# Gate-tile sums tied to a place in VectorE's queue, and pooling blocks spread over projection blocks, in a one-core transformer block

## The chip, the cores and the metric

The kernel runs on one core of one Trainium2 chip. The metric is the time of one execution in device microseconds (us); three executions of the kernel before the change gave 2939.7, 2941.09 and 2943.04, median 2941.09. One more execution was recorded by the profiler and is the source of every row below.

## The reference, cut to what matters

One layer of a diffusion backbone in float32, with 256 latent tokens, 256 context tokens and 4096 channels:

```
mod  = silu(c) @ w_ada + b_ada              -> shift, scale, gate    (w_ada: 4096 x 12288)
h    = rmsnorm(x) * (1 + scale) + shift     (the context likewise, from c_ctx)
xa, xb, ga, gb = split(h @ w_in)            (w_in: 4096 x 16384; the context needs xa alone)
ya   = RG-LRU(xa): convolution, two gates per head and direction, two scans (16 heads)
z    = centred_mean(xb, window 2, 4, 8, 16) - xb      (4 groups of 1024 channels)
yb   = (z @ w_pool[group] + b_pool) * pool_scale
x    = x + gate * ([ya * silu(ga), yb * silu(gb)] @ w_out)           (w_out: 8192 x 4096)
out  = rmsnorm(x) * g_final
```

## The kernel before

Float32 weights are split on the core into two float32r tiles. `load_w` (L101 to L109) starts a transfer of one 128x1024 weight tile into a `raw` buffer on SyncE's queue (L97), lets ScalarE write the high half `hi` (L104) and VectorE the low half `lo = raw - hi` (L106; for the first 139 tiles GpSimd does it). TensorE multiplies with `hi` and with `lo`. There are 9 buffers for `raw`, 4 for `hi` and 3 for `lo` (`RAWB, HIB, LOB`). A weight tile is called a unit here; the kernel has 843 of them.

The whole program is one list of events, which `run` walks: "w" events eat a weight tile, "a" events eat a tile that goes straight into a sum, "s" events do other work. `run` loads 5 weight tiles (`LOOK`) and 4 "a" tiles (`LOOK_A`) ahead. A scheduler then places the recorded instructions in each engine's queue; it keeps dependencies, but may put an instruction earlier or later than it was written. Each engine takes its own queue in order, so an instruction that waits holds up all that is queued behind it on that engine.

After a first stage (up to about 860 us, the same in both kernels) come two stages:

- **Projection** (to 2196 us). A block is 8 units that fill two PSUM tiles (`block_units`, matmuls L613 and L614); there are 16 blocks for `xb`, 16 for `gb`, 16 for `ga`. The blocks of `xb` come in four groups; each block's result is folded and pooled on ScalarE and VectorE (`evac_x`) into eight tiles `z` per group. A group's pooling products are four blocks of two units each (`prods`, weights `w_pool`, the same lines L613 and L614, reading `z`); each fills two PSUM tiles, which a copy on ScalarE (L587) and an addition on VectorE (L592) then empty into `yb`. There are four PSUM tiles for these blocks in all (`ps_mm`). A group's four pooling blocks stand in a row after the first `DELAY` = 12 units of the next group. The LRU pieces of 16 heads are spread over the whole stage; each has two weight tiles of its own (L522 to L524).
- **Output** (2196 to 2921 us). 8 blocks of 32 units (`out_units`); a unit is twelve matmuls, four each on L796 (high half), L797 (low half) and L798.

The gate vector is computed on VectorE: 4 groups of 32 tiles of `w_ada`, each tile multiplied by one column and added into a `wide` tile (`gate_units`, `accumulate`, L223, L225, and L231 for the last tile). Group 0 is spread over the end of the projection, groups 1 to 3 over 0.03 to 0.83 of the output stage (`GATE3`). A group's result is needed late, at unit 24 of the output block that uses it (`gate_row`, L762).

Of the kernel before, what the change touches and what calls it, by code (L numbers as in the profile page):

```python
# [15 lines left out]
KT = D // P  # L16
# [1 line left out]
T2 = 2 * T  # L18
HEADS = 16
KEEP = 8  # L20
DELAY = 12
GATE3 = (0.03, 0.83)
GATE_FROM, GATE_END = 0.9, 0.99
SPILL_Y = 12
GATE_AT = 24
# [17 lines left out]
W = 1024  # L43
# [25 lines left out]
def block_kernel(ctx, tc, xc, cvec, vecs, consts, w_ss, w_gate, w_xa, w_lat0, w_lat2, w_lat, w_pool, w_rec, w_out, xn, rows, out):  # L69
# [13 lines left out]
    def slot(name, dt=F32):  # L83
        return spool.tile([P, 512], dt, name=name, tag="s")

    def temp(name, dt=F32):
        return tpool.tile([P, 512], dt, name=name, tag="t")
# [4 lines left out]
    def wide_tile():  # L92
        return ps_2.tile([P, 1024], F32, name="wide", tag="wide")

    def load_raw(src):
        t = rawp.tile([P, W], F32, name="raw", tag="raw")[:, :src.shape[-1]]
        nc.sync.dma_start(out=t, in_=src)  # L97
        return t

    def load_w(src, eng=None):  # L100
        raw = load_raw(src)  # L101
        width = src.shape[-1]
        hi = hip.tile([P, W], F32R, name="hi", tag="hi")[:, :width]
        act.copy(out=hi, in_=raw)  # L104
        lo = lop.tile([P, W], F32R, name="lo", tag="lo")[:, :width]
        ins = (eng or dve).tensor_tensor(out=lo, in0=raw, in1=hi.bitcast(F32), op=SUB)  # L106
        if eng is not None:
            lo_ins.append(ins)
        return hi, lo  # L109

    lo_ins, used = [], [0]

    def run(events):
        queues = {}
        for kind, look in (("w", LOOK), ("a", LOOK_A)):
            queues[kind] = [[e for e in events if e[0] == kind], [], 0, look]
        for e in events:
            if e[0] == "s":
                e[1]()
                continue  # L120
            for kind in ("w", "a"):
                q = queues[kind]
                q[2] += e[0] == kind
                while len(q[1]) < min(len(q[0]), q[2] + q[3]):
                    n = q[0][len(q[1])]
                    q[1].append(load_w(n[1], n[3]) if kind == "w" else load_raw(n[1]))
            q = queues[e[0]]
            r, q[1][q[2] - 1] = q[1][q[2] - 1], None
            e[2](r)
# [4 lines left out]
    def A_(src, f):  # L134
        return ("a", src, f)

    def S_(f):
        return ("s", f)
# [79 lines left out]
    def accumulate(raw, j, width, k, accs, nv, part, fins, first, last):  # L218
        seg = raw[:, j * width:(j + 1) * width]
        for v in range(nv):  # L220
            s = sc6[:, k, 2 + v:3 + v]
            if first:
                dve.tensor_scalar(out=accs[v][:, :width], in0=seg, scalar1=s, scalar2=None, op0=MUL)  # L223
            elif not last:
                dve.scalar_tensor_tensor(out=accs[v][:, :width], in0=seg, scalar=s, in1=accs[v][:, :width],  # L225
                                         op0=MUL, op1=ADD)
            else:
                for h in range(width // part):
                    fin = temp("fin")
                    cut = slice(h * part, (h + 1) * part)  # L230
                    dve.scalar_tensor_tensor(out=fin[:, :part], in0=seg[:, cut], scalar=s, in1=accs[v][:, cut],  # L231
                                             op0=MUL, op1=ADD)
                    fins[h, v] = fin
# [43 lines left out]
    def gate_units(grp):  # L277
        st = {}

        def unit(k):  # L280
            def f(raw):
                if k == 0:
                    st["accs"] = [wide_tile()]
                    st["fin"] = {}
                accumulate(raw, 0, W, k, st["accs"], 1, 512, st["fin"], k == 0, k == KT - 1)
            return A_(w_gate[grp, k], f)

        return [unit(k) for k in range(KT)], st
# [41 lines left out]
    ya_sp = [dram.tile([P, 512], F32, name=f"ya_sp{h}") for h in range(HEADS)]  # L330

    def xa_units(c):
        k0, n = chunk_kt[c]
        per = W // n // P

        def unit(i):
            def f(w):
                used[0] += 1
                hi, lo = (t.rearrange("p (k m) -> p k m", k=n) for t in w)
                for j in range(per):  # L340
                    o = i * per + j
                    ps = mm_tile()
                    for k in range(n):
                        a, b = hc[k0 + k]
                        wh, wl = hi[:, k, j * P:(j + 1) * P], lo[:, k, j * P:(j + 1) * P]
                        pe.matmul(out=ps, lhsT=wh, rhs=a, start=(k == 0), stop=False)  # L346
                        pe.matmul(out=ps, lhsT=wh, rhs=b, start=False, stop=False)  # L347
                        pe.matmul(out=ps, lhsT=wl, rhs=a, start=False, stop=(k == n - 1))  # L348
                    if c == 0:
                        acc[o] = slot("acc")  # L350
                        act.copy(out=acc[o], in_=ps)
                    elif c < NC - 1 and o % 4 < POOL_ADDS:
                        part = temp("part")
                        act.copy(out=part, in_=ps)  # L354
                        nc.gpsimd.tensor_tensor(out=acc[o], in0=acc[o], in1=part, op=ADD)  # L355
                    else:
                        dve.tensor_tensor(out=acc[o], in0=ps, in1=acc[o], op=ADD)
                    if c == NC - 1 and o >= 2 * KEEP:
                        nc.sync.dma_start(out=xa_sp[o], in_=acc[o])
                        acc[o] = None  # L360
            return W_(w_xa[xa_base[c] + i], f, nc.gpsimd)
        return [unit(i) for i in range(32 // per)]
# [96 lines left out]
    for c in range(NC):  # L459
        main = xa_units(c)  # L460
        if c == 0:
            main = spread(main, ahead_units())
        if c == NC - 1:
            events.append(S_(softplus))
        if c + 1 < NC:
# [8 lines left out]
            if c > 0:  # L474
                side = [spill_ahead(b) for b in range((c - 1) * SPILLS, min(AHEAD, c * SPILLS))]
                loads = [load_x(k) for k in range(k1, k1 + n1)]
                main = spread(main, spread(side, loads, 0.2, 1.0) if side else loads, 0.0, 0.6)
# [142 lines left out]
    yb = [None] * 16  # L620
    ya = [None] * 16
# [53 lines left out]
    def gated_units(base, ymix, spilled):  # L675
        units = []
        early = {}

        def fetch(blk):
            def f():  # L680
                early[blk] = temp("early")
                nc.sync.dma_start(out=early[blk], in_=ahead_sp[base + blk - AHEAD_FROM])
            return S_(f)

        def evac(blk):
            def f(j, ps):
                if j == 0 and spilled is not None:
                    ymix[blk] = slot("ya2") if blk < 12 else temp("ya3")
                    nc.sync.dma_start(out=ymix[blk], in_=spilled[blk])
                v, s = temp("gv"), temp("gs")  # L690
                fold(ps, v[:, 0:T])
                if blk in early:
                    dve.tensor_tensor(out=v[:, 0:T], in0=v[:, 0:T], in1=early[blk][:, j * T:(j + 1) * T], op=ADD)
                act.activation(out=s[:, 0:T], in_=v[:, 0:T], func=AF.Sigmoid)
                dst = ymix[blk][:, j * T:(j + 1) * T]
                dve.tensor_tensor(out=v[:, 0:T], in0=v[:, 0:T], in1=s[:, 0:T], op=MUL)
                dve.tensor_tensor(out=dst, in0=dst, in1=v[:, 0:T], op=MUL)
            return f

        for blk in range(16):  # L700
            e = base + blk - AHEAD_FROM
            if e < 0:
                units += block_units([w_lat[base + blk, i] for i in range(8)], hT, evac(blk))
            else:
                srcs = [w_lat2[e]] + [w_lat[base + blk, i] for i in range(1, 8)]
                u = block_units(srcs, hT, evac(blk), 2)
                units += u[:4] + [fetch(blk)] + u[4:]
        return units

    main, late = [], []  # L710
    for g in range(4):
        units, prods = pool_units(g)
        main += units[:DELAY] + late + units[DELAY:]
        late = prods
    units = gated_units(16, yb, None)
    main += units[:DELAY] + late + units[DELAY:] + gated_units(32, ya, ya_sp)
    rec = []
    prev = []
    for h in range(HEADS):
# [94 lines left out]
    main = spread(out_units(0), [make_mix(n) for n in range(4, 32)], 0.0, 28 / 34)  # L814
    main += [u for blk in range(1, 8) for u in out_units(blk)]
    events += spread(main, [u for grp in range(1, 4) for u in gates[grp][0]], GATE3[0], GATE3[1])

    run(events)

    for n in range(SPILL_Y):  # L820
# [4 lines left out]
    tot, w, r = (tiny[:, 2 * n:2 * n + 2] for n in range(3))  # L825
# [96 lines left out]
```

## Time and profile before

| | |
|---|---|
| median of three executions | 2941.09 us (2939.7 to 2943.04) |
| the profiled execution's own time | 2941.93 us |
| its span, first to last instruction | 2940.1 us |
| TensorE busy | 2854.3 us (97%) |
| mean granted TensorE clock | 0.993 of full speed |

The span is what the trace shows; 1.8 us of the execution's own time lie around it. Each engine's rows have a start, a duration and, in square brackets, how long the engine had been idle before and what ended that. TensorE's matmuls overlap, so two rows that follow each other without a wait start closer together than one row is long.

### The profile page before, as it was taken

The page shows a single profiled execution, that of the slowest core. Times are in us where ns is not written, and L with a number is a line of the kernel's source. Part 1 is how long each engine was busy: PE and PEld are TensorE (multiplying, and loading weights), DVE is VectorE, ACT ScalarE, POOL GpSimd, SP SyncE. Part 2 cuts the span into 40 slices and gives each one's busy share as a digit, 9 for nine tenths or more (in the row PEclk, how much of TensorE's full clock was granted, in tenths as well). Part 3 has the DMA queues.
Part 4 walks back from the last instruction along what each step waited for, and adds up shares of the span by engine and source line. Part 5 has one row for each costly group of instructions (what it writes and reads, how often), then busy time and mean ns, then how long its engine had stood idle before and what let it go on. Part 6 is the DMA issues. An engine that isn't in the chain of part 4 may idle for free.

```text
span 2940.1 us, 38457 instructions
## 1 busy us (share of the span) xinstructions
PE 2854.3 (97%) x13946; PEld 2349.6 (80%) x13946; DVE 2221.4 (76%) x2667; ACT 1551.6 (53%) x2105; POOL 585.0 (20%) x345
## 2 busy tenths in 40 slices
PE   6999999999999999999999999999999999999997
PEld 2777777877878888888888888888888877777886
DVE  5899999988277777878677678777999766656554
ACT  4544433444346656766666676677664433333333
POOL 1567777877820000000000000000000000000000
PEclk9999999999999999999999999999999999999998
DMA  8997778776445555555555566666999887787773
GB/s 336 380 334 274 287 284 294 289 263 241 146 159 175 168 175 170 176 183 179 168 187 184 181 197 195 205 206 201 331 335 342 304 290 269 263 281 277 268 241 125
DMA packets 211583, 702.95 MB, mean 239 GB/s; under 512 B 23616, under 2 KB 23744, under 8 KB 211392
## 3 DMA queue, kind: packets, MB, share of 16 engines
q1 hardware_dynamic: 202752, 684.75, 67.5%
q10 hardware_dynamic: 8640, 15.73, 1.5%
q8 instruction: 109, 1.79, 0.2%
q14 instruction: 82, 0.67, 0.1%
HBM read 678.90 MB, written 21.50 MB: 238 GB/s over the span
## 4 chain that ended last, share of the span: by engine, by line
PE 89%; DVE 4%; DMA 4%; issue 1%; ACT 1%; POOL 1%; SPq 0%; DVEq 0%; ACTq 0%; POOLq 0%
PE mm L613 25%; PE mm L614 13%; PE mm L797 7%; PE mm L346 7%; PE mm L798 7%; PE mm L796 7%; PE mm L347 7%; PE mm L348 7%; PE wide L524 2%; PE wide L522 2%; PE wide L523 2%; DMA raw<-in_w_gate 2%; PE mm L249 1%; DVE lo L106 1%; DVE wide L225 1%
## 5 line engine op out<-in xcount | busy, mean ns | idle before, releaser
L104 ACT CAST hi<-raw 128x1024 fp32r<-128x1024 f32 x843 | 874.2, 1039 | 945.6 <-PE mm L798 372.7
L106 DVE TENSOR_TENSOR lo<-raw,hi 128x1024 fp32r<-128x1024 f32 (+1 forms) x704 | 842.1, 1205 | 329.3 <-PE mm L614 121.3
L613 PE MATMUL mm<-hT,hi 128*128 128x512 f32 x2984 | 1055.1, 398 | 0.0
L614 PE MATMUL mm<-hT,lo 128*128 128x256 f32 x2984 | 837.7, 281 | 0.0
L225 DVE SCALAR_TENSOR_TENSOR wide<-raw,sc,wide 128x1024 f32<-128x1024 f32 (+1 forms) x592 | 693.0, 1229 | 156.6 <-DMA raw<-in_w_gate 143.5
L613 PEld LDWEIGHTS mm<-hT,hi 128*128 128x128 f32 x2984 | 560.6, 188 | 139.2
L614 PEld LDWEIGHTS mm<-hT,lo 128*128 128x128 f32 x2984 | 563.6, 189 | 1.3
L346 PE MATMUL mm<-hhi,hi 128*128 128x512 f32 x1024 | 402.5, 394 | 14.0 <-ACT hhi L141 8.9
L797 PE MATMUL mm<-lo,mix 128*128 128x512 f32 x1024 | 400.9, 392 | 15.3 <-DVE lo L106 15.1
L347 PE MATMUL mm<-hlo,hi 128*128 128x512 f32 x1024 | 400.7, 392 | 2.5 <-DVE hlo L142 2.5
L796 PE MATMUL mm<-hi,mix 128*128 128x512 f32 x1024 | 401.8, 392 | 0.0
L348 PE MATMUL mm<-hhi,lo 128*128 128x512 f32 x1024 | 399.9, 391 | 0.0
L798 PE MATMUL mm<-hi,mix 128*128 128x512 f32 x1024 | 398.9, 390 | 0.0
L106 POOL TENSOR_TENSOR lo<-raw,hi 128x1024 fp32r<-128x1024 f32 x139 | 334.4, 2406 | 192.2 <-POOL acc L355 61.0
L346 PEld LDWEIGHTS mm<-hhi,hi 128*128 128x128 f32 x1024 | 192.9, 189 | 66.0 <-ACT hhi L141 10.8
L797 PEld LDWEIGHTS mm<-lo,mix 128*128 128x128 f32 x1024 | 192.2, 188 | 65.3 <-DVE lo L106 24.5
L355 POOL TENSOR_TENSOR acc<-acc,part 128x512 f32<-128x512 f32 x168 | 215.6, 1297 | 69.8 <-ACT part L354 68.4
L347 PEld LDWEIGHTS mm<-hlo,hi 128*128 128x128 f32 x1024 | 193.2, 189 | 44.8 <-DVE hlo L142 5.8
L796 PEld LDWEIGHTS mm<-hi,mix 128*128 128x128 f32 x1024 | 192.2, 188 | 42.0 <-issue 1.9
L348 PEld LDWEIGHTS mm<-hhi,lo 128*128 128x128 f32 x1024 | 193.1, 189 | 40.2
L798 PEld LDWEIGHTS mm<-hi,mix 128*128 128x128 f32 x1024 | 192.2, 188 | 39.4
L354 ACT COPY part<-mm 128x512 f32<-128x512 f32 x168 | 98.1, 584 | 163.0 <-PE mm L348 156.0
(143 smaller groups left out, 2439.9 us busy)
## 6 DMA issues: line engine op xcount, KB each, us to landing
raw<-in_w_lat SPq DMA_DIRECT2D x373, 512.0 KB, 3.6
raw<-in_w_ss SPq DMA_DIRECT2D x256, 512.0 KB, 5.0
raw<-in_w_out SPq DMA_DIRECT2D x256, 512.0 KB, 4.8
raw<-in_w_xa SPq DMA_DIRECT2D x128, 512.0 KB, 4.5
raw<-in_w_gate SPq DMA_DIRECT2D x128, 512.0 KB, 4.9
raw<-in_w_rec SPq DMA_DIRECT2D x32, 512.0 KB, 3.5
raw<-in_w_pool SPq DMA_DIRECT2D x32, 512.0 KB, 3.5
x<-in_xc SPq DMA_DIRECT2D x32, 256.0 KB, 7.0
```

The costliest lines, as they stand in the source:

```text
L104: act.copy(out=hi, in_=raw)
L106: ins = (eng or dve).tensor_tensor(out=lo, in0=raw, in1=hi.bitcast(F32), op=SUB)
L225: dve.scalar_tensor_tensor(out=accs[v][:, :width], in0=seg, scalar=s, in1=accs[v][:, :width], op0=MUL, op1=ADD)
L346: pe.matmul(out=ps, lhsT=wh, rhs=a, start=(k == 0), stop=False)
L347: pe.matmul(out=ps, lhsT=wh, rhs=b, start=False, stop=False)
L348: pe.matmul(out=ps, lhsT=wl, rhs=a, start=False, stop=(k == n - 1))
L355: nc.gpsimd.tensor_tensor(out=acc[o], in0=acc[o], in1=part, op=ADD)
L613: pe.matmul(out=ps, lhsT=hi[:, k, m], rhs=a, start=first, stop=False)
L614: pe.matmul(out=ps[:, 0:T], lhsT=lo[:, k, m], rhs=a[:, 0:T], start=False, stop=last)
L796: pe.matmul(out=ps, lhsT=mh, rhs=hi[:, k], start=(i == 0 and k == 0), stop=False)
L797: pe.matmul(out=ps, lhsT=mh, rhs=lo[:, k], start=False, stop=False)
L798: pe.matmul(out=ps, lhsT=ml, rhs=hi[:, k], start=False, stop=(i == 31 and k == 1))
```

## The change

Three things. (1) The sum of a gate tile gets an edge that queues it on VectorE behind one low half: with n weight tiles eaten, that of tile n + 1 counted from 0 (`PIN` = 1), two after the tile eaten last. To this end `load_w` keeps the low half's instruction of every weight tile, and `run` keeps the count in `eaten`. (2) `DELAY` goes; `mixed` puts a pooling block of two units behind the sixth unit of each of the next group's four projection blocks. (3) The last gate groups end at 0.8 of the output stage where it was 0.83.

```diff
-DELAY = 12
-GATE3 = (0.03, 0.83)
+LATE_AT = 5
+GATE3 = (0.03, 0.8)
+PIN = 1
...
         ins = (eng or dve).tensor_tensor(out=lo, in0=raw, in1=hi.bitcast(F32), op=SUB)
-        if eng is not None:
-            lo_ins.append(ins)
+        lo_ins.append(ins)
         return hi, lo
 
-    lo_ins, used = [], [0]
+    lo_ins, used, eaten = [], [0], {}
...
                 q[2] += e[0] == kind
+                eaten[kind] = q[2]
...
-                accumulate(raw, 0, W, k, st["accs"], 1, 512, st["fin"], k == 0, k == KT - 1)
+                with tc.issue_after(lo_ins[min(eaten["w"] + PIN, len(lo_ins) - 1)].ins):
+                    accumulate(raw, 0, W, k, st["accs"], 1, 512, st["fin"], k == 0, k == KT - 1)
...
+    def mixed(units, late):
+
+        out, n = [], 0
+        starts = [u for u, e in enumerate(units) if e[0] == "w"][::8]
+        for u, e in enumerate(units):
+            out.append(e)
+            if late and u == starts[n] + LATE_AT:
+                out += late[:2]
+                late = late[2:]
+                n += 1
+        return out + late
+
     main, late = [], []
     for g in range(4):
         units, prods = pool_units(g)
-        main += units[:DELAY] + late + units[DELAY:]
+        main += mixed(units, late)
         late = prods
-    units = gated_units(16, yb, None)
-    main += units[:DELAY] + late + units[DELAY:] + gated_units(32, ya, ya_sp)
+    main += mixed(gated_units(16, yb, None), late) + gated_units(32, ya, ya_sp)
```

How the instructions move is seen at three places. Names carry a number that grows in the order in which tiles are loaded.

VectorE's queue in the output stage, before (`raw_21531` is a gate tile, the others are weight tiles):

```order
L106 TENSOR_TENSOR lo_21372<-raw_21368,hi_21370 128x1024
L225 SCALAR_TENSOR_TENSOR wide_21424<-raw_21531,sc6_90,wide_21424 128x1024
L106 TENSOR_TENSOR lo_21390<-raw_21386,hi_21388 128x1024
L106 TENSOR_TENSOR lo_21408<-raw_21404,hi_21406 128x1024
L770 TENSOR_TENSOR ov_21477<-mm_20852,gb_21294 128x512
L771 TENSOR_TENSOR y_21338<-y_21338,ov_21477 128x512
L106 TENSOR_TENSOR lo_21430<-raw_21426,hi_21428 128x1024
```

and after the change, in the same stretch (`raw_21408` and `raw_21465` are gate tiles):

```order
L107 TENSOR_TENSOR lo_21523<-raw_21519,hi_21521 128x1024
L226 SCALAR_TENSOR_TENSOR wide_21370<-raw_21408,sc6_90,wide_21370 128x1024
L107 TENSOR_TENSOR lo_21541<-raw_21537,hi_21539 128x1024
L107 TENSOR_TENSOR lo_21562<-raw_21558,hi_21560 128x1024
L226 SCALAR_TENSOR_TENSOR wide_21370<-raw_21465,sc6_90,wide_21370 128x1024
L107 TENSOR_TENSOR lo_21582<-raw_21578,hi_21580 128x1024
L107 TENSOR_TENSOR lo_21603<-raw_21599,hi_21601 128x1024
```

Before, the sum of a gate tile stood ahead of the low half of a weight tile that was loaded long before it; now it stands behind the low halves of weight tiles that were loaded after it.

SyncE's queue, which issues the transfers of those tiles, before:

```order
L97 DMA raw_21386<-in_w_out 128x1024
L97 DMA raw_21404<-in_w_out 128x1024
L97 DMA raw_21422<-in_w_gate 128x1024
L97 DMA raw_21426<-in_w_out 128x1024
L97 DMA raw_21444<-in_w_out 128x1024
L97 DMA raw_21462<-in_w_gate 128x1024
L97 DMA raw_21465<-in_w_out 128x1024
L822 DMA y_25252<-y_sp0_433 128x512
L97 DMA raw_21493<-in_w_out 128x1024
L97 DMA raw_21513<-in_w_out 128x1024
L97 DMA raw_21531<-in_w_gate 128x1024
```

and after:

```order
L98 DMA raw_21465<-in_w_gate 128x1024
L98 DMA raw_21468<-in_w_out 128x1024
L98 DMA raw_21496<-in_w_out 128x1024
L98 DMA raw_21516<-in_w_gate 128x1024
L773 DMA gb_21944<-in_rows 128x512
L98 DMA raw_21519<-in_w_out 128x1024
L765 DMA y_21988<-in_xn 128x512
L98 DMA raw_21537<-in_w_out 128x1024
L98 DMA raw_21555<-in_w_gate 128x1024
L98 DMA raw_21558<-in_w_out 128x1024
```

Before, seven weight tiles (`raw_21386` to `raw_21513`) are issued ahead of gate tile `raw_21531`, and their low halves stand behind its sum. After, the sum of `raw_21465` stands behind the low halves of five weight tiles that are issued after it (`raw_21468` to `raw_21558`).

SyncE's queue at the first pooling products, which shows the order in which TensorE takes the tiles as well, before:

```order
L97 DMA raw<-in_w_lat 128x1024 x4
L97 DMA raw<-in_w_rec 128x1024
L97 DMA raw<-in_w_lat 128x1024 x6
L97 DMA raw<-in_w_pool 128x1024 x8
L97 DMA raw<-in_w_rec 128x1024
L97 DMA raw<-in_w_lat 128x1024 x5
```

and after:

```order
L98 DMA raw<-in_w_lat 128x1024 x4
L98 DMA raw<-in_w_rec 128x1024
L98 DMA raw<-in_w_pool 128x1024 x2
L98 DMA raw<-in_w_lat 128x1024 x8
L98 DMA raw<-in_w_pool 128x1024 x2
L98 DMA raw<-in_w_lat 128x1024 x2
L98 DMA raw<-in_w_rec 128x1024
L98 DMA raw<-in_w_lat 128x1024 x6
```

Eight pooling units in a row became pairs, with eight projection units between one pair and the next.

## Rows read from the trace of the kernel before

**Rows 1.** The page's first part: busy time of each engine over the span.

```profile
PE 2854.3 (97%) x13946; PEld 2349.6 (80%) x13946; DVE 2221.4 (76%) x2667; ACT 1551.6 (53%) x2105; POOL 585.0 (20%) x345
```

**Rows 2.** Windows of the output stage: busy us (instructions), clock, DMA share, GB/s.

```profile
core 0: us, PE busy (x) PEld busy (x) DVE busy (x) ACT busy (x) POOL busy (x), PEclk, DMA share, GB/s
...
2300.00:2400.00 100.00, 99.98 (x439) 82.06 (x438) 66.56 (x60) 39.68 (x41) 0.00 (x0) 1.00 0.87 302
2400.00:2500.00 100.00, 93.45 (x402) 74.53 (x401) 59.60 (x54) 36.40 (x38) 0.00 (x0) 1.00 0.76 266
2500.00:2600.00 100.00, 97.64 (x428) 79.85 (x427) 63.91 (x58) 38.20 (x40) 0.00 (x0) 1.00 0.82 279
2600.00:2700.00 100.00, 95.80 (x413) 76.41 (x412) 62.36 (x57) 36.94 (x38) 0.00 (x0) 1.00 0.79 273
2700.00:2800.00 100.00, 97.79 (x427) 79.70 (x426) 57.93 (x54) 38.23 (x40) 0.00 (x0) 1.00 0.76 259
2800.00:2900.00 100.00, 100.00 (x439) 82.07 (x439) 49.59 (x45) 40.09 (x41) 0.00 (x0) 1.00 0.64 214
```

**Rows 3.** Waits of TensorE over the span: us in total, times, longest.

```profile
PE mm L797 <- DVE lo L106: 15.1, 15, 2.7
...
PE mm L613 <- DVE yb L592: 7.1, 4, 4.2
...
PE wide L524 <- DVE lo L106: 1.0, 1, 1.0
```

**Rows 4.** Waits of VectorE from 2200 to 2760 us, the longest.

```profile
DVE wide L225 <- DMA raw<-in_w_gate: 143.5, 54, 4.9
```

**Rows 5.** Timeline of VectorE in the output stage.

```profile
2493.70 1.29 DVE L225 SCALAR_TENSOR_TENSOR wide<-raw,sc,wide 128x1024 f32<-128x1024 f32 x1 [4.92 <-DMA raw<-in_w_gate]
2494.89 3.49 DVE L106 TENSOR_TENSOR lo<-raw,hi 128x1024 fp32r<-128x1024 f32 x3
```

**Rows 6.** Timeline of TensorE at the same place.

```profile
2492.82 0.39 PE L798 MATMUL mm<-hi,mix 128*128 128x512 f32 x1
2493.05 0.39 PE L796 MATMUL mm<-hi,mix 128*128 128x512 f32 x1
2496.17 0.50 PE L797 MATMUL mm<-lo,mix 128*128 128x512 f32 x1 [2.73 <-DVE lo L106]
2496.50 0.40 PE L798 MATMUL mm<-hi,mix 128*128 128x512 f32 x1
```

**Rows 7.** Timeline of TensorE between the first and second pooling block.

```profile
1016.03 0.28 PE L614 MATMUL mm<-z,lo 128*128 128x256 f32 x1
1020.55 0.77 PE L613 MATMUL mm<-z,hi 128*128 128x512 f32 x1 [4.25 <-DVE yb L592]
...
1021.33 0.63 PE L613 MATMUL mm<-z,hi 128*128 128x512 f32 x1
...
1021.97 0.63 PE L613 MATMUL mm<-z,hi 128*128 128x512 f32 x1
...
1023.80 0.39 PE L613 MATMUL mm<-z,hi 128*128 128x512 f32 x1
...
1024.15 0.39 PE L613 MATMUL mm<-z,hi 128*128 128x512 f32 x1
```

**Rows 8.** Timeline of ScalarE at the same place.

```profile
1018.62 1.06 ACT L104 CAST hi<-raw 128x1024 fp32r<-128x1024 f32 x1
1019.55 0.67 ACT L587 COPY fold<-mm 128x256 f32<-128x256 f32 x2
```

**Rows 9.** Windows at the first pooling wait and where gate group 0 is loaded.

```profile
1015.00:1025.00 10.00, 5.75 (x25) 4.76 (x24) 4.71 (x8) 9.94 (x15) 0.00 (x0) 0.83 0.40 136
...
2120.00:2140.00 20.00, 20.00 (x115) 17.31 (x114) 20.00 (x25) 9.44 (x13) 0.00 (x0) 1.00 0.99 362
2140.00:2160.00 20.00, 20.00 (x115) 17.35 (x114) 18.81 (x26) 9.80 (x15) 0.00 (x0) 1.00 1.03 403
```

**Rows 10.** Transfers: weight tiles from 2400 to 2740 us (median us to landing).

```profile
raw<-in_w_out SPq DMA_DIRECT2D x116, 512.0 KB, 4.9
```

**Rows 11.** All transfers that line L97 issues, over the span.

```profile
DMA to landing us min/median/max: 2.6/4.4/10.5
```

## The prediction

> **What bounds the kernel now.** I read the page's busy times first, then TensorE's waits over the span, then windows of the stage in which most of them lie, then the timelines of single waits on the engine that waits and on the one waited for. TensorE is busy for 97% of the span [rows 1], so only its waits and its slow stretches can be won; no other engine is near. Of the waits that the change touches, two lines carry nearly all: matmul L797 waits for a low half, 15.1 us in 15 waits, and matmul L613 of the pooling products waits for VectorE's addition into `yb`, 7.1 us in 4 waits, with 1.0 us for one low half among the pooling units [rows 3]. The windows show where the first lie: a quiet stretch holds 439 matmuls in 100 us, the four from 2400 to 2800 us hold 402, 428, 413 and 427 [rows 2]. VectorE is busy for some 60 of 100 us there, so it is not short of time: it stands still. Its own wait is for gate transfers, 143.5 us in 54 waits [rows 4]. One of them in full: VectorE idles 4.92 us until a gate tile lands, sums it in 1.29 us, and then makes three overdue low halves in a row [rows 5]; TensorE, which needed the first, lost 2.73 us [rows 6]. The order shows why: the sum was queued ahead of the low halves of seven weight tiles whose transfers were issued before its own.
>
> **Part 1, the sums tied to low halves.** What goes: in rows 2 the four windows hold 1670 matmuls where 4 x 439 = 1756 would fit; 86 x 0.228 us (100 / 439) = **19.6 us**. The timeline agrees: 15 waits of 15.1 us, and each costs about 0.27 us more than its wait, because undisturbed matmuls start 0.23 us apart though one lasts 0.39, an overlap that a wait breaks [rows 6]; 15.1 + 4.1 = 19.2. I take 19.6.
>
> What comes: a sum now stands behind the low half two tiles ahead, so the low halves that TensorE needs next are already made when it runs. Gate tiles are loaded four ahead, one per two weight tiles (96 sums over some 194 units), so a sum follows its transfer's issue by some 4 x 2 + 2 = 10 units, about 27 us at 12 x 0.228 = 2.73 us a unit. The slowest transfer of the span landed in 10.5 us [rows 11]. The wait of rows 4 should go almost whole. The work stays: per unit one low half of 1.16 us (3.49 / 3) and half a sum of 1.29 [rows 5], 1.8 of 2.73 us on VectorE.
>
> The price is in the buffers. A gate tile holds its `raw` buffer for 10 units, so five of nine are gate tiles, and a weight tile's transfer can start only when the low half four or five tiles earlier is done; SyncE's queue, in which such a transfer waits for its buffer, keeps that order and passes nothing over. A turn of this ring is transfer 4.9 us [rows 10], high half 1.06 [rows 8], a sum that may stand between 1.29 and a low half 1.16 [rows 5], and some 0.4 us of issue and semaphores (my allowance): 8.8 us, against 4.5 x 2.73 = 12.3 us in which TensorE eats as many tiles. It keeps up with 3.5 us to spare; price taken: 0.
>
> Group 0, at the end of the projection, is denser: 32 sums among 46 units, and in the buffers that the changed program assigns a ring of three tiles for some 14 units. A projection unit is eight pairs of 0.35 us [rows 7], 2.8 us, so three give 8.4 us for a turn of 8.8 or more: some 0.4 us late per turn, up to 2 us late if the ring is slowed as much as the crowded stretch suggests. From below: before the change that stretch already ran at 362 to 403 GB/s with VectorE busy 20.00 and 18.81 of 20 us, and TensorE lost nothing [rows 9]. From above: five turns at 2 us, less the two tiles (5.6 us) that are always made ahead, gives 4.4. I take **+2 us**, between the two.
>
> **Part 2, pooling blocks inside projection blocks.** Before, a pooling block began on the PSUM tiles that the one before it had just filled, since the half-done projection block held the other two. The wait of rows 7: the last matmul starts at 1016.03, the copy that empties the tile starts at 1019.55, behind other ScalarE work [rows 8], and TensorE resumes at 1020.55, 4.25 us idle. It resumed at half pace: pairs 0.64 us apart, and 0.35 from 1023.80 on [rows 7]; five pairs in 3.25 us instead of 1.77 cost 1.5 us. The granted clock of that window is 0.83 [rows 9], a mixture of 2.4 and 1.2 GHz. So the sum is: waits 7.1 + 1.0 us [rows 3], 5 x 0.27 = 1.4 for broken overlap, and 2 x 1.5 = 3.0 for the slow pairs behind the two waits over 2 us: **12.4 us**.
>
> After, two units separate a pooling block from the projection block that takes over its tiles: at least 2 x 2.8 = 5.6 us, and a tile is needed again only as long after as the other of its pair, which makes it about 7. The latest emptying so far took 4.5 us from the last matmul's start to the restart [rows 7]. So all five waits end; price left: 0, and at worst a few us where a run of ScalarE work as in rows 9 (9.94 of 10 us busy) falls on a copy. The products now begin six units (17 us) after their group's last projection block instead of twelve; the `z` chain of copies and additions has that time, and slots for `z` are held longer, which delays VectorE at most as long as its next low half waits anyway.
>
> **Part 3.** 96 tiles over 0.77 instead of 0.80 of the stage is 4% more load per unit, inside the 3.5 us to spare: 0, if that margin goes, it is rival 3. `gate_row` uses the last group some 18 units after its last sum.
>
> **The clock in the output stage.** Its windows read 1.00 throughout [rows 2], so a wait there costs its length and 0.27 us, no slow pairs. The Trainium skill (TensorE: Matmul & The Clock Gate, "A second HAM failure mode: psum-queue depth-cycling") says that short idle times that recur between groups of matmuls can make the clock swing between its two levels, which costs throughput beyond the idle time. By that rule the 15 waits would hide another 15 x 1.5 us and the gain would be 22 us larger; the trace does not agree here.
>
> **Sum.** 2941.9 (the profiled execution) - 19.6 - 12.4 + 2.0 = 2911.9. It was 0.8 us above the median of three, so a median of about **2911 us**. A measurement of this kernel tells about 0.2% (6 us) from no change.
>
> **Rivals.**
> 1. *The pooling waits only move.* Sixteen pooling blocks now each put copies and additions on ScalarE and VectorE beside a projection block's own; 0.8 us lost at each would give back the 12.4 us: 2923. For it: ScalarE's crowding in rows 9. Against: the spare 2.5 us per block.
> 2. *Only half of the output waits go*, because weight tiles land late in some turns: 2911 + 10 = 2921. Against: 3.5 us to spare.
> 3. *Slower: the ring of weight buffers becomes the bound.* Each weight tile then waits for its transfer. It decides from a turn of 12.3 us, a landing time of 8.4 us; at 10.5 us, the slowest seen [rows 11], a turn is 14.4 us, 3.2 us a unit, (3.2 - 2.73) x 194 = 91 us lost: 2911 + 91 = 3002. The break-even with before is a loss of 30 us, a landing time of about 9.1 us. Against: 4.9 us was the median with more transfers queued [rows 10]. The Trainium skill (Perfetto Trace Analysis, "Optimization Strategy") reads bubbles that repeat over a stretch as a sign of too few buffers for the next tile; by that rule the waits of rows 2 would grow when gate tiles take buffers, and this rival would come true. Rows 4 speak against it: before, the engine stood still for the order of its queue.
> 4. *The edge or the new places change nothing that TensorE feels*: 2941. Against: the order shows both moved.
> 5. *The output waits do carry slow pairs that the windows round away*: 2911 - 22 = 2889.
>
> **Chances.** Forecast 0.70 (2904 to 2918), rival 1 0.11, rival 2 0.09, rival 3 0.04, rival 4 0.04, rival 5 0.02. The range leaves out rivals 3 to 5, 0.10, and takes in both halves: 2904 (the group 0 price gone, with the spread of executions) to 2927 (rival 1 with the 4.4 us bound). Faster by over 0.2%: 0.70 + 0.11 + 0.09 + 0.02 = 0.92; within 0.2%: 0.04; slower: 0.04.
>
> **What would show it.** Right: L797's waits for a low half near 0, VectorE's waits for gate transfers gone, windows of 2400 to 2700 us at 438 or more matmuls, the clock at 1.00 around the pooling blocks, no wait of L613 for `yb`, the output stage starting some 10 us earlier. Wrong: waits of ScalarE's high half for `raw<-in_w_out` over 10 us in the output stage (rivals 2, 3), L613 waiting for a `fold`, `gv` or `z` (rival 1), TensorE gaps where group 0 is loaded (the +2 too small).

## The result and the profile after

The changed kernel took 2905.6 us (median of four, 2902.47 to 2906.88) against 2941.73 (four runs of the kernel before): a ratio of 0.9874, 95% interval 0.9862 to 0.9885, some 36 us. The profiled execution took 2906.24 us with a span of 2904.4.

The stages can be cut by the first and last start of their matmuls. Ahead of the comma stand count and duration (ns), behind it the first and last start in us. Of the kernel before, by line:

```profile
L613 PE MATMUL mm<-hT,hi x2984: 389/398/403, 864.3 to 2195.5; 128*128 128x512 f32 x199
...
L796 PE MATMUL mm<-hi,mix x1024: 387/389/791, 2195.8 to 2920.4; 128*128 128x512 f32 x171
...
L798 PE MATMUL mm<-hi,mix x1024: 387/389/402, 2196.3 to 2920.9; 128*128 128x512 f32 x171
```

Of the changed kernel (two lines lower for the projection, thirteen for the output):

```profile
L615 PE MATMUL mm<-hT,hi x2984: 389/398/403, 861.4 to 2181.7; 128*128 128x512 f32 x199
...
L809 PE MATMUL mm<-hi,mix x1024: 389/389/791, 2182.0 to 2884.9; 128*128 128x512 f32 x171
...
L811 PE MATMUL mm<-hi,mix x1024: 388/389/397, 2182.5 to 2885.3; 128*128 128x512 f32 x171
```

| us, from the starts above | before | after | forecast |
|---|---|---|---|
| first stage (to the first L613) | 864.3 | 861.4 | same |
| projection (to the first L796) | 1331.5 | 1320.6 | -12.4 + 2.0 |
| output, from 2195.8 or 2182.0 to its last start + 0.4 | 725.5 | 703.7 | -19.6 |
| tail to the end of the span | 18.8 | 18.7 | same |

The two stages that the change touches gave 10.9 + 21.8 = 32.7 us. The remaining 2.9 us of this pair lie in the first stage, whose instructions are the same (see the last section).

TensorE's waits over the span, the lines that answer to [rows 3] (L616 is L614 before): nothing is left of the waits of L797 (now L810) for a low half and of L613 (L615) for `yb`; one new wait has come. The wait of the LRU's weight tile (L524) for a low half is gone as well.

```profile
PE mm L250 <- DMA raw<-in_w_ss: 21.2, 13, 10.0
PE mm L348 <- ACT hhi L142: 8.9, 2, 7.4
...
PE mm L616 <- DVE lo L107: 0.8, 1, 0.8
```

The windows of the output stage, against [rows 2]: full everywhere, 441 matmuls in every 100 us (439 where two `gate_row`s fall into one window, as at 2508 and 2597 us), and from 2400 to 2700 a higher transfer rate than before, because TensorE eats faster. From 2700 on the rate is lower, 241 for 259 GB/s: with the earlier end fewer gate tiles are left.

```profile
2300.00:2400.00 100.00, 100.00 (x441) 82.45 (x440) 68.62 (x61) 40.31 (x41) 0.00 (x0) 1.00 0.87 305
2400.00:2500.00 100.00, 100.00 (x441) 82.43 (x440) 67.32 (x59) 39.34 (x40) 0.00 (x0) 1.00 0.85 292
2500.00:2600.00 100.00, 100.00 (x439) 82.05 (x438) 68.06 (x61) 39.23 (x40) 0.00 (x0) 1.00 0.84 290
2600.00:2700.00 100.00, 100.00 (x441) 82.45 (x440) 69.84 (x61) 40.25 (x41) 0.00 (x0) 1.00 0.84 294
2700.00:2800.00 100.00, 100.00 (x441) 82.45 (x440) 56.62 (x54) 39.92 (x43) 0.00 (x0) 1.00 0.70 241
```

The window from 2300 to 2400 us of the kernel before, with 439 matmuls [rows 2], held one `gate_row` as well. The two that it lacks went to a low half that came late, by too little to be listed as a wait; undisturbed, these two would start 0.23 us apart:

```profile
2371.77 0.39 PE L796 MATMUL mm<-hi,mix 128*128 128x512 f32 x1
2372.18 0.50 PE L797 MATMUL mm<-lo,mix 128*128 128x512 f32 x1
```

VectorE's waits from 2160 to 2760 us, against [rows 4]: no gate transfer is on the list. It waits for TensorE to give a `lo` buffer back, that is, it is ahead.

```profile
DVE lo L107 <- PE mm L810: 130.7, 88, 1.5
DVE lo L107 <- issue: 31.2, 81, 1.8
```

The same seen singly, VectorE's timeline in that stage, against [rows 5]: a low half at the moment a buffer comes free, the sum right behind it and without a wait of its own, the next low half 2.72 us after the one before. That is TensorE's pace of one unit.

```profile
2489.40 1.23 DVE L107 TENSOR_TENSOR lo<-raw,hi 128x1024 fp32r<-128x1024 f32 x1 [1.50 <-PE mm L810]
2490.55 1.28 DVE L226 SCALAR_TENSOR_TENSOR wide<-raw,sc,wide 128x1024 f32<-128x1024 f32 x1
2492.12 1.22 DVE L107 TENSOR_TENSOR lo<-raw,hi 128x1024 fp32r<-128x1024 f32 x1 [0.29 <-issue]
2494.84 1.23 DVE L107 TENSOR_TENSOR lo<-raw,hi 128x1024 fp32r<-128x1024 f32 x1 [1.50 <-PE mm L810]
```

Around a pooling block, against [rows 9]: TensorE 30 of 30 us busy, the clock at 1.00.

```profile
985.00:1015.00 30.00, 30.00 (x165) 25.77 (x164) 22.25 (x31) 17.22 (x23) 0.00 (x0) 1.00 0.52 175
...
2100.00:2120.00 20.00, 19.18 (x109) 16.43 (x108) 19.22 (x26) 9.44 (x13) 0.00 (x0) 1.00 0.91 303
```

The second line is where the new wait lies: gate group 0, VectorE 19.22 of 20 us busy. The wait can be followed back over three engines:

```profile
2093.64 1.05 ACT L105 CAST hi<-raw 128x1024 fp32r<-128x1024 f32 x1 [0.98 <-DMA raw<-in_w_lat]
2094.72 1.23 DVE L107 TENSOR_TENSOR lo<-raw,hi 128x1024 fp32r<-128x1024 f32 x1 [0.91 <-ACT hi L105]
2104.42 0.39 PE L616 MATMUL mm<-hT,lo 128*128 128x256 f32 x1 [0.82 <-DVE lo L107]
```

A gate sum gave a buffer back at 2088.33 us, the next weight tile's transfer into it started at 2088.36 and landed at 2093.56, and VectorE stood still for 0.91 us until its high half was made. From there on VectorE had no pause up to the low half that it began at 2103.17 us, and for this one TensorE waited 0.82 us.

### The profile page after: what moved, and what is told of

It reads as the page before. It is cut to its first block, busy times and chain, and to the rows that moved or that the text cites. A ratio compares the mean times of both kernels' runs of the same rounds, so it can differ in the third digit from the quotient of the medians.

```text
span 2904.4 us, 38437 instructions
## 1 busy us (share of the span) xinstructions
PE 2841.8 (98%) x13946; PEld 2349.2 (81%) x13946; DVE 2227.7 (77%) x2667; ACT 1552.4 (53%) x2105; POOL 584.7 (20%) x345
## 4 chain that ended last, share of the span: by engine, by line
PE 92%; DVE 3%; DMA 2%; issue 1%; ACT 1%; POOL 0%; SPq 0%; ACTq 0%; DVEq 0%
PE mm L615 26%; PE mm L616 13%; PE mm L809 8%; PE mm L811 8%; PE mm L810 8%; PE mm L348 7%; PE mm L349 7%; PE mm L350 7%; PE wide L524 2%; PE wide L525 2%; PE wide L526 2%; PE mm L250 1%; DMA x<-in_xc 1%; DVE wide L226 1%; DMA raw<-in_w_ss 1%
## 5 line engine op out<-in xcount | busy, mean ns | idle before, releaser
L615 PE MATMUL mm<-hT,hi 128*128 128x512 f32 x2984 | 1055.9, 399 | 0.0
L616 PE MATMUL mm<-hT,lo 128*128 128x256 f32 x2984 | 838.0, 281 | 0.8 <-DVE lo L107 0.8
L615 PEld LDWEIGHTS mm<-hT,hi 128*128 128x128 f32 x2984 | 560.6, 188 | 139.3
L616 PEld LDWEIGHTS mm<-hT,lo 128*128 128x128 f32 x2984 | 563.6, 189 | 2.6 <-DVE lo L107 1.4
L810 PE MATMUL mm<-lo,mix 128*128 128x512 f32 x1024 | 398.3, 389 | 0.0
L348 PEld LDWEIGHTS mm<-hhi,hi 128*128 128x128 f32 x1024 | 192.8, 188 | 65.8 <-ACT hhi L142 10.9
L810 PEld LDWEIGHTS mm<-lo,mix 128*128 128x128 f32 x1024 | 192.2, 188 | 41.6 <-issue 1.9
```

The lines of the kernel that those rows point to most:

```text
L615: pe.matmul(out=ps, lhsT=hi[:, k, m], rhs=a, start=first, stop=False)
L616: pe.matmul(out=ps[:, 0:T], lhsT=lo[:, k, m], rhs=a[:, 0:T], start=False, stop=last)
L810: pe.matmul(out=ps, lhsT=mh, rhs=lo[:, k], start=False, stop=False)
```

## The experiments

The theory: three parts at separate places; the sums paid because VectorE stood still for gate tiles that had not landed, the pooling blocks because each began on PSUM tiles that had just been filled, and the earlier end pays nothing. Rivals: the parts need each other; the gain over the forecast comes from the earlier end; the buffers that gate tiles now hold are about to become the bound.

### Each part alone

`pin_only` keeps the edge and takes the rest back:

```diff
+DELAY = 12
 LATE_AT = 5
-GATE3 = (0.03, 0.8)
+GATE3 = (0.03, 0.83)
...
-        main += mixed(units, late)
+        main += units[:DELAY] + late + units[DELAY:]
...
-    main += mixed(gated_units(16, yb, None), late) + gated_units(32, ya, ya_sp)
+    units = gated_units(16, yb, None)
+    main += units[:DELAY] + late + units[DELAY:] + gated_units(32, ya, ya_sp)
```

> Part 1 alone: the edge on the gate sums, pooling blocks and the end at 0.83 as before. Theory (the parts act at separate places and add up): the output stage, from the first L796-type matmul to the last, shrinks from 725.4 to about 704 us, the pooling waits of 7.1 us stay, some 1 us is lost where gate group 0 is loaded: 2941.7 - 21.7 + 1 = 2921 us. Rival A (the edge needs the thinner or denser gate spacing of 0.8 to pay): the output stage keeps over 5 us of waits for low halves, 2927 or more. Rival B (ring of weight buffers binds): ScalarE's high halves wait for w_out transfers, over 2930.

`mixed_only` keeps the pooling places, without the edge and with the end at 0.83:

```diff
-GATE3 = (0.03, 0.8)
+GATE3 = (0.03, 0.83)
...
-                with tc.issue_after(lo_ins[min(eaten["w"] + PIN, len(lo_ins) - 1)].ins):
+                if True:
                     accumulate(raw, 0, W, k, st["accs"], 1, 512, st["fin"], k == 0, k == KT - 1)
```

> Part 2 alone: pooling blocks inside projection blocks, no edge, end at 0.83. Theory: the projection stage shrinks from 1331.5 to about 1320 us, the waits of the pooling matmuls for VectorE's addition into yb are 0, the output stage keeps its 15 us of waits for low halves: 2941.7 - 11.5 = 2930 us. Rival (the pooling waits only move): 2936 to 2942.

`end08_only` is the kernel before with one number changed:

```diff
-GATE3 = (0.03, 0.83)
+GATE3 = (0.03, 0.8)
```

> Part 3 alone: the last gate groups end at 0.8, no edge, pooling blocks as before. Theory: nothing is won, since the sums still stand ahead of low halves; the waits of the output stage are packed into a stage 4% shorter: 2941 us, at most 1 us either way. Rival (the 6 us by which the change beat the sum come from the earlier end): 2936.

`pin_mixed_083` is the changed kernel without that number:

```diff
-GATE3 = (0.03, 0.8)
+GATE3 = (0.03, 0.83)
```

> Parts 1 and 2 without part 3 (end at 0.83). Theory: 2905.6 us, within 2 of the whole change, TensorE without waits in the output stage. Rival (part 3 carries what the sum missed): 2911.

Measured against 15 runs of the kernel before on the same chip (2940.68 us):

| kernel | us | ratio, 95% interval | projection us | output us |
|---|---|---|---|---|
| `pin_only` | 2915.36 | 0.9913, 0.9900 to 0.9927 | 1332.9 | 703.7 |
| `mixed_only` | 2927.45 | 0.9952, 0.9940 to 0.9965 | 1319.7 | 722.3 |
| `end08_only` | 2940.05 | 0.9999, 0.9990 to 1.0008 | 1332.1 | 729.4 |
| `pin_mixed_083` | 2906.09 | 0.9882, 0.9867 to 0.9897 | 1320.8 | 703.7 |

(The stages are those of each kernel's profiled execution, cut as above.) The theory holds. Each stage answers to its own part alone: the output stage is 703.7 us with the edge and 722 to 729 without it, the projection 1320 with the new places and 1332 without. The totals of `pin_only` and `mixed_only` were 6 and 3 us below what was expected. For `pin_only` the two stages are as expected; its profiled execution had a first stage of 857.4 us, 6.9 us shorter than that of the kernel before. In `mixed_only` the output stage was 3 us shorter, with 11.4 us of waits where there were 15.1. Against 2940.68 the two alone add up to 38.5 us, and both together (`pin_mixed_083`) gave 34.6; the intervals are some 4 us wide to either side and don't tell the two apart. The end at 0.8 wins nothing: alone it left TensorE 16.7 us of waits for low halves, its output stage was even 4 us longer, and without it the change is as fast.

The traces of `mixed_only` and `end08_only` also show what that of the kernel before did not: slow matmuls behind waits in the output stage. In `mixed_only`, the matmuls behind one wait of 2.48 us started 0.43 us apart instead of 0.23, and the granted clock of that window of 10 us was 0.83:

```profile
2477.00:2487.00 10.00, 7.52 (x26) 5.71 (x26) 6.33 (x6) 2.10 (x2) 0.00 (x0) 0.83 0.71 262
```

```profile
2480.82 0.66 PE L810 MATMUL mm<-lo,mix 128*128 128x512 f32 x1 [2.48 <-DVE lo L107]
2481.27 0.63 PE L811 MATMUL mm<-hi,mix 128*128 128x512 f32 x1
2481.70 0.63 PE L809 MATMUL mm<-hi,mix 128*128 128x512 f32 x1
...
2484.57 0.39 PE L810 MATMUL mm<-lo,mix 128*128 128x512 f32 x1
2484.80 0.39 PE L811 MATMUL mm<-hi,mix 128*128 128x512 f32 x1
```

Twelve matmuls from there took 4.45 us, where they take 2.85 behind a wait at the full clock: 1.6 us lost. In `end08_only` two waits, of 2.06 and 2.32 us, were followed by the same, 1.6 and 1.3 us lost; that is most of its 4 us.

TensorE's waits in `mixed_only` show the stalls of the output stage without the edge, none of pooling:

```profile
PE mm L250 <- DMA raw<-in_w_ss: 18.7, 13, 8.1
PE mm L810 <- DVE lo L107: 11.4, 13, 2.5
```

and in `pin_only` the reverse:

```profile
PE mm L616 <- DVE yb L595: 7.1, 4, 4.3
...
PE wide L527 <- DVE lo L108: 1.0, 1, 1.0
...
PE mm L617 <- DVE lo L108: 1.0, 1, 1.0
```

The waits of [rows 3] for `yb` and for the low half of the LRU weights are both back. VectorE's first wait from 2160 to 2760 us in `mixed_only` is again for gate transfers:

```profile
DVE wide L226 <- DMA raw<-in_w_gate: 140.7, 52, 4.7
```

### How late a sum has to stand

The edge was moved five and nine low halves ahead, all else as in the changed kernel.

```diff
-PIN = 1
+PIN = -4
```

> The whole change with the edge five low halves earlier (PIN = -4): sums of groups 2 and 3 stand 5 places earlier in VectorE's queue, about 5 units (13.7 us) behind their transfer's issue, and the ring is 6 tiles. Theory (all that matters is that the sum comes later than its tile lands, 4.9 us): as the whole change, 2904 to 2908 us, no waits for gate transfers. Rival (low halves two ahead are what pays): waits for low halves come back, over 2912.

```diff
-PIN = 1
+PIN = -8
```

> The whole change with the edge nine low halves earlier (PIN = -8): a sum comes about one unit, 2.7 us, behind its transfer's issue, less than the 4.9 us of landing. Theory: VectorE waits some 2 us per gate tile again, part of it reaches TensorE, 5 to 12 us of waits for low halves, 2912 to 2920 us. Rival (any edge that keeps the order helps): 2906 us.

`pin_m4` took 2903.91 us (0.9874, 0.9857 to 0.9890), `pin_m8` 2904.09 (0.9876, 0.9862 to 0.9891); both have an output stage of 703.7 us. The first is as expected, the second is not: no wait of TensorE for a low half came back. In both, TensorE's wait at gate group 0 is gone too, and the projection took 1319.7 us. In VectorE's waits of `pin_m8` from 2160 to 2760 us, sums do not appear:

```profile
DVE lo L107 <- PE mm L810: 115.4, 78, 1.5
DVE lo L107 <- issue: 32.1, 74, 1.8
DVE lo L107 <- DMA raw<-in_w_out: 10.7, 8, 1.5
DVE lo L107 <- DMA raw<-in_w_gate: 6.0, 4, 1.5
```

I had counted from the event list how far ahead a gate tile is loaded. What counts is when its transfer can start: when the last reader of its buffer is done, a low half or another sum. So I counted, in the programs' order and buffers, how many low halves stand on VectorE from that reader to the sum. For groups 2 and 3 (64 tiles) it is 1 or 2 before the change (60 tiles), 3 to 5 in `pin_m8` (59), 5 to 8 in `pin_m4` (63), 8 to 12 in the changed kernel (all). The trace of the kernel before shows the cliff by itself, when each of the 96 sums of groups 1 to 3 is set beside its count:

| low halves from the reader to the sum | sums | of them waited for their transfer | wait on average, us |
|---|---|---|---|
| 1 | 23 | 23 | 3.3 |
| 2 | 39 | 34 | 1.9 |
| 3 or more | 34 | 0 | 0 |

In `pin_m8`, `pin_m4` and the changed kernel 4, 1 and 0 sums have a count of 2, none has 1, and none of the 96 waited. At 2.73 us each, 1 or 2 low halves are 2.7 to 5.5 us, against a landing time of 4.9 [rows 10]; 3 are 8.2. So here the cliff lies between two and three low halves. It also says why TensorE had no listed wait before 2400 us: 30 of the 32 tiles of group 1 have 3 or more. All three places tried, -8, -4 and 1, serve, and the one chosen is on the safe side; that it lets the two next low halves go first is not what pays.

### How many buffers the change can spare

```diff
-RAWB, HIB, LOB = 9, 4, 3
+RAWB, HIB, LOB = 8, 4, 3
```

> The whole change with 8 raw buffers instead of 9: a weight tile's transfer then waits for the low half 4 tiles earlier all through the output stage. Theory (a turn of the ring takes 8.8 us, against 4 x 2.73 = 10.9 us of TensorE): nothing is lost in the output stage, 703 us long; 1 to 3 us more where gate group 0 is loaded; 2906 to 2909 us. Rival (the ring already binds or is about to): output stage over 708 us.

```diff
-RAWB, HIB, LOB = 9, 4, 3
+RAWB, HIB, LOB = 7, 4, 3
```

> The whole change with 7 raw buffers: a ring of 3 weight tiles, 8.2 us of TensorE against a turn of 7.8 us (sum in every second turn) to 8.8 us (sum in every turn). Theory: the ring becomes the bound or is close to it, output stage 10 to 40 us longer than 703, ScalarE's high halves wait for w_out transfers, 2916 to 2945 us; projection (3.6 us landing, few sums) nearly unchanged. Rival (buffers are not what the change pays with): 2906 us.

`raw8` took 2913.61 us (0.9906, 0.9891 to 0.9921), `raw7` 2923.94 (0.9942, 0.9928 to 0.9957): over the first range and inside the second, but not for the reason given. The output stage is 703.7 and 703.8 us, as with 9 buffers. With 7 buffers the ring is three tiles: 175 of 176 weight tiles there (2220 to 2700 us) go into a buffer that was given back three low halves earlier. ScalarE's waits of `raw7` from 2160 to 2760 us show that this ring is near its limit:

```profile
ACT hi L105 <- DMA raw<-in_w_out: 229.5, 136, 4.2
ACT hi L105 <- PE mm L811: 77.5, 53, 2.6
```

With 9 buffers the first of these two was 7.1 us, in 4 waits. ScalarE now waits for a transfer at most tiles, but TensorE doesn't feel it. So a turn of the ring is on average at most 3 x 2.73 = 8.2 us, inside the 7.8 to 8.8 expected, while the loss of 10 to 40 us in the output stage didn't come. What fewer buffers cost lies elsewhere. The first L615 starts at 865.8 and 870.7 us in `raw8` and `raw7`, later than in every execution with 9 buffers (857.4 to 864.3, see the last section). The projection is 1322.5 and 1327.8 us instead of 1320.6, where TensorE's waits in `raw7` include

```profile
PE mm L616 <- DVE lo L107: 4.4, 8, 1.1
```

of which 3.9 us in 7 waits lie behind 2000 us, where gate group 0 is loaded.

### Other places for the pooling blocks

```diff
-LATE_AT = 5
+LATE_AT = 2
```

> The whole change with the pooling blocks behind the third unit of a projection block instead of the sixth (LATE_AT = 2): 8.5 us sooner after their group's last projection block. In the change's trace the last z of the four groups was written 15.3, 7.4, 11.6 and 5.2 us before the first pooling product, which needs it one unit (2.8 us) later still. Theory (the products have that much time and no more): the group with 5.2 us waits about 0.5 to 1 us, the others nothing, projection stage 1320 to 1324 us, 2905 to 2910 us. Rival (z is made just in time for whatever stands ahead of it): 4 waits of several us, over 2915.

```diff
-LATE_AT = 5
+LATE_AT = 7
```

> The whole change with the pooling blocks behind the last unit of a projection block (LATE_AT = 7): two units between the end of one projection block and the next, about 7 us to empty its tiles; the pooling tiles then have 8 units. Theory (what counts is that no block begins on tiles that were filled a moment ago): as the whole change, projection stage 1319 to 1323 us, 2904 to 2908 us. Rival (the emptying of a projection block, longer than that of a pooling block, does not fit into 7 us): L615 waits for a fold or pad again, over 2910.

`late2` took 2906.3 us (0.9886, 0.9871 to 0.9902) with a projection of 1321.4, `late7` 2905.71 (0.9887, 0.9868 to 0.9905) with 1319.3. Both totals are as expected. In `late2` one group's `z` came too late:

```profile
PE mm L615 <- DVE z L143: 0.7, 1, 0.7
```

It is not the group that was expected to wait. The wait, at 1111.64 us, is in the second group, which had a margin of 7.4 us: its products began at 1104.69 instead of 1120.03, 15.3 us sooner and not 8.5, because an LRU piece (5.5 us) that stood ahead of them now stands behind. The fourth group, with 5.2 us, moved by 8.9 us and didn't wait. So a place inside the block will do, if it leaves about two units for a block's tiles to be emptied and `z` the time to be made.

### Two attempts to win more

`m4_from08` thins gate group 0 out, with the edge of `pin_m4`:

```diff
-GATE_FROM, GATE_END = 0.9, 0.99
+GATE_FROM, GATE_END = 0.8, 0.99
...
-PIN = 1
+PIN = -4
```

> The whole change with the edge of pin_m4 and gate group 0 spread over 0.8 to 0.99 of the projection instead of 0.9 to 0.99, 32 sums among twice as many units. Theory (the 1.3 us lost at group 0 come from its density): those go, projection 1319 us, 2904 us. Rival (tiles held longer in the projection stage shorten its ring): projection over 1322 us.

`raw10_hi3` gives one buffer of high halves to the raw tiles:

```diff
-RAWB, HIB, LOB = 9, 4, 3
+RAWB, HIB, LOB = 10, 3, 3
```

> The whole change with one raw buffer more and one buffer for high halves less (10, 3, 3). With 8 and 7 raw buffers the first stage ended 4 and 9 us later than with 9. Theory (the first stage lives on raw buffers, the later ones have spare high halves): the first stage ends 2 to 4 us earlier, output stage 703 us still, 2901 to 2904 us. Rival (three high halves bring ScalarE's cast behind TensorE): waits of TensorE for high halves, over 2910.

Neither won. `m4_from08` took 2909.15 us (0.9897, 0.9880 to 0.9913), its projection 1322.9 where that of `pin_m4` was 1319.7: a wait for a low half (0.9 us), which `pin_m4` doesn't have, and small ones for `wide` tiles (1.4) and high halves (0.6) came, so its rival was nearer. `raw10_hi3` took 2908.89 (0.9895, 0.9880 to 0.9910); its first stage ended at 864.2 us, at the late end of the executions with 9 buffers and not ahead of them, so a tenth raw buffer at the price of a high half brings nothing there. Its output stage was 703.7 us again. No version tried is clearly faster than the change: `pin_m4` and `pin_m8`, 1.7 and 1.5 us below it in the median, overlap with it in interval.

## Why the prediction was right

It forecast 2911 us (2904 to 2927) and the likeliest case came, with 36 us won where 30 were forecast. That the time lies near the lower end of the range is in part chance, by the 2.9 us of the first stage. By its steps:

- **The sums.** The mechanism was right: queue order, not VectorE's time or the transfers' rate. The place behind the low half two tiles ahead was more than was needed: three low halves behind the buffer's release are enough, as the table shows. The size was a little off, 21.8 us measured for 19.6. The term took 439 matmuls as the quiet rate; a quiet window with one `gate_row` holds 441, and the one that was read had lost two to the late low half at 2372.18. Against 441 in each, the four windows of [rows 2] lack 94 matmuls, 21.3 us. By starts, 19.2 us are the 15 listed waits with the overlap that they broke, as the prediction had it, and 1.8 us more are 13 late starts like the one above.
- **The price in buffers, 0 for groups 1 to 3.** Right, with more to spare than the working said: it estimated a turn of 8.8 us; `raw7` ran the output stage at full pace with a ring of three, so at 8.2 us or less. No run shows the 0.4 us of issue and semaphores as such: in the chain at gate group 0 above, the gaps between release, issue, landing, high half and low half add up to 0.14 us. The Trainium skill (Perfetto Trace Analysis, "Optimization Strategy") says that bubbles that repeat over a stretch can mean too few buffers for the next tile. These bubbles did not mean that: with two buffers fewer than the kernel before, and the right order, they were gone.
- **Gate group 0, +2.** There was a new wait, 0.8 us in the waits, 1.1 us with the starts around it, so about half of the term. The chain above begins as the prediction said, with a weight tile that waited for its buffer; the full VectorE then carried the delay on. Where the sums give their buffers back earlier, in `pin_m4` and `pin_m8`, the wait is gone.
- **The pooling blocks, 12.4.** 10.9 + 1.1 = 12.0 us by the difference of the stages, 11.8 by `mixed_only`. The slow pairs behind two waits, the part that rows of the clock gave, belonged in the sum: waits and overlap alone are 9.5.
- **The earlier end, 0.** Right by both runs on it.
- **The clock in the output stage.** Right for the execution that was read: behind none of its 15 waits did the matmuls run slower, and rival 5 (22 us more) is out. As a statement on such waits it was partly luck: in `mixed_only` one of 13 and in `end08_only` two of 16 waits like them were followed by slow matmuls, at 1.3 to 1.6 us each.

What the forecast did not have: 2.9 of the 35.7 us between the two profiled executions lie in the first stage. What is left between the 32.7 us of the stages and the 36 of the medians can't be assigned: it may be the same scatter, or slow matmuls in other executions of the kernel before. The mean granted clock of the 15 executions of the kernel before that were measured with `pin_only` was 0.991 to 0.993; the profiled one, without slow matmuls in the output stage, had 0.993, and `end08_only`, with two such stretches there, 0.991.

## What to carry to other kernels

When an engine that is only 60% busy holds up a full one, look at what stands ahead in its queue: an instruction that a scheduler moved early, onto data that is still in flight, blocks all that is ready behind it. One ordering edge mends it; count how many instructions lie between the reader that frees the buffer and the new reader, multiply by the pace, and compare with the landing time. Here the sums waited up to two places behind that reader and not from three on. And place short blocks that fill PSUM where enough other work, here two units (5.6 us), separates them from whoever takes over their tiles.

## What the runs showed of the hardware

- **The first stage scatters.** In ten profiled executions with the same first stage (9, 4, 3 buffers, `m4_from08` left aside) the first matmul of the projection started between 857.4 and 864.3 us, though the order of instructions ahead of it was the same; TensorE's waits there for `in_w_ss` transfers were 18.6 to 21.4 us. That is over half of the smaller of the two effects studied here, so a stage's own length is the better measure of a part.
- **Waits of like length, two clocks.** Behind the wait of 4.25 us, and one of 2.40 us at 1426.10, the pairs of [rows 7] ran at half pace, and the granted clock of 10 us around each was 0.83. In the output stage the pace fell behind waits of 2.06, 2.32 and 2.48 us (`end08_only`, `mixed_only`), but stayed full, with a clock of 1.00, behind waits of 2.73 us [rows 6] and 2.17 us (`end08_only`, at 2578.84). So the length of the wait alone doesn't decide; these runs don't show what does.
- **A transfer that waits for its buffer starts at once.** In the output stage of the changed kernel and of `raw7`, the transfer of a weight tile started 0.03 us (median) after the last reader of its buffer had ended.
